# A transformer forward pass in split float32: two matmuls (512 and 256 columns) in place of three (256 each) per weight tile in the transposed projections

## The chip, the cores and the metric

The kernel runs on one core of a Trainium2 chip. The metric is the device time of one execution in microseconds; a time is the median of several executions. TensorE multiplies, VectorE and ScalarE move results out of the accumulator banks (PSUM) and do the element work, GpSimd does small numerics, and SyncE (SP) issues the loads of the weights.

## What is computed

256 tokens of 2048 channels pass through two attention layers (one with an index-selected key set, one plain causal), a block that mixes sparse attention (NSA) with a gated delta rule, and a gated feed-forward network (FFN). All is float32. Nearly all the work is projections, activations times a weight matrix that is read once. The ones that the change touches are marked:

```python
gate = h @ w_in[:, 3072:5120]                 # touched, in both attention layers
h = h + (silu(gate) * o) @ w_out
proj = rms_norm(h, norm1_w) @ w_in_2          # touched: delta rule's q, k, v and the merge gates
mixed = g_nsa * (o_nsa @ w_up_nsa) + g_dn * (o_dn @ w_up_dn)     # touched, both
x = h + mixed @ w_o
h2 = rms_norm(x, norm2_w)
x = x + (silu(h2 @ w_ffn_gate) * (h2 @ w_ffn_up)) @ w_ffn_down   # touched: gate and up
```

## The kernel before

Activations are kept transposed, 128 channels on the partitions, in blocks of 4 x 128 channels by 256 tokens, and each block twice: `hi`, rounded to the matmul's float32r, and `lo`, what the rounding left. The weights stream through once. For each 1 MB load `raw` (512 rows by 512 columns, three buffers, issued by SP at L134) ScalarE casts a half of it to `wh` (L139) and VectorE subtracts to get `wl` (L140); each has three buffers. A product is then high·high + low·high + high·low, three matmuls into one bank.

`gemm` (L121) has two forms. Unflipped, the activations are the stationary operand and 512 weight columns move (L155 to L157). Flipped (`flip=True`), a 128 x 128 tile of weights is stationary and 256 tokens move (L148 to L150), so that the result comes out transposed. A flipped call has two banks; each holds two blocks of 128 columns by 256 tokens, and at the end of the call each bank is evacuated by one VectorE instruction of 512 columns, a multiplication by a per-token row (L573, L1255, L1265, L1327, L1335) or, after the up-projections of the two mixers, an add-and-multiply (L1278, L1290). The tag `mm` has four banks, so that two calls overlap.

There are 52 flipped calls: 44 with four input blocks (8 attention gates, 6 for the delta rule's q, k, v, 8 merge gates, 11 FFN gates, 11 FFN ups) and 8 short ones with two (four each for `w_up_nsa_2` and `w_up_dn_2`). The FFN runs in three passes, over 4, 4 and 3 column blocks of its inner width; a pass is its gate and up calls, then unflipped down calls.

Other work (attention, top-k, delta rule, sparse attention) runs in generators that `tick` advances between the matmuls of the projections, and `defer` puts small pieces some ticks later. `need(name)` runs a generator to its end before the next line is written. A scheduler then orders each engine's queue, so the order on an engine is near to that of the code but not the same. On one engine the queue is worked off in order. `split_into` (L521) splits a result into `hi` and `lo`; `x_T` (L238) transposes a residual block for the next layer on TensorE (L219) and splits it (L233, L234); `row_of` (L166) spreads per-token factors over the partitions.

Of the kernel before, what the change touches and what calls it, by code (L numbers as in the profile page):

```python
# [11 lines left out]
F32 = mybir.dt.float32  # L12
F32R = mybir.dt.float32r
# [13 lines left out]
class Kern:  # L27
    """The whole forward pass; activations stay in SBUF, weights stream through once."""

    def __init__(self, ctx, tc, d, out, stop=None):  # L30
# [9 lines left out]
        self.flip = False  # L40
        self.finished = set()

# [4 lines left out]
    def ev(self, name, dt=F32):  # L47
        """evacuations of the projections, apart from the background's tiles"""
        return self.sb.tile([P, 512], dt, tag="ev", bufs=8, name=name)

    def slot(self, name, dt=F32):
        """a [128, 2, 512] tile in a slot of the split activations"""
        self.flip = not self.flip
        return self.sb.tile([P, 2, 512], dt, tag="hi" if self.flip else "lo", bufs=8, name=name)
# [20 lines left out]
    def defer(self, n, fn):  # L75
        """trace fn after n further ticks"""
# [15 lines left out]
    def tick(self):  # L92
        """advance deferred work and the background chains"""
# [27 lines left out]
    def gemm(self, xT, W, c0, n, evac, ng=4, split=False, flip=False):  # L121
# [3 lines left out]
        pt = [self.ps.tile([P, 512], F32, tag="mm", bufs=4, name="mm") for _ in range(2)]  # L125
        for g in range(ng):
# [8 lines left out]
            hi, lo = xT[g]  # L135
            for h in range(2):
                wh = self.sb.tile([P, 2, n], F32R, tag="wh", bufs=3, name="wh")
                wl = self.sb.tile([P, 2, n], F32R, tag="wl", bufs=3, name="wl")
                nc.scalar.copy(wh, raw[:, 2 * h:2 * h + 2])  # L139
                nc.vector.tensor_tensor(wl, raw[:, 2 * h:2 * h + 2], wh.bitcast(F32), ALU.subtract)  # L140
                for c in range(2):
# [1367 lines left out]
```

## Time and profile before

| | |
|---|---|
| runs | 2311.62, 2310.85, 2311.79 us; median 2311.62 |
| span of the profiled execution, first to last instruction | 2308.8 us |
| TensorE matmul / weight load busy | 2295.5 us (99%) / 2094.7 us (91%) |
| VectorE / ScalarE / GpSimd busy | 1395.8 us (60%) / 1089.4 us (47%) / 133.6 us (6%) |
| matmuls | 16446 |
| read from memory, mean rate | 397.95 MB, 174 GB/s over the span |

The page gives no other time for the profiled execution than its span; the runs are 2.1 to 3.0 us above it. A line of the profile names the engine, the line of the kernel, the operation, what it writes and reads, a count, the busy time and the mean of one; "PEld" is TensorE's load of stationary weights. A matmul is drawn from its start to the end of its passage through the array, and the next one begins before that, so a step from one matmul to the next is shorter than a matmul.

### The profile page before, as it was taken

To read this page: it belongs to the slowest core of one execution; us is meant where nothing else is said; L and a number is where in the kernel's file an instruction comes from. 1 tells how busy PE (TensorE), PEld (TensorE's weight loads), DVE (VectorE), ACT (ScalarE), POOL (GpSimd) and SP (SyncE) were. 2 spreads that over 40 slices of the span, in tenths; PEclk is the share of its full clock that TensorE was granted. 3 is DMA by queue.
4 is the path that set the end of the run, shared out by engine and by line. 5 is a ranking of instruction groups with operands and counts; after the bars stand their busy time and mean duration, and the time that the engine had idled before them with its cause. 6 is when DMAs were issued, how large, how long until landed. Compare 5 with 4: busy or idle time off the path is not lost.

```text
span 2308.8 us, 39431 instructions
## 1 busy us (share of the span) xinstructions
PE 2295.5 (99%) x16446; PEld 2094.7 (91%) x16446; DVE 1395.8 (60%) x2073; ACT 1089.4 (47%) x1758; POOL 133.6 (6%) x233
## 2 busy tenths in 40 slices
PE   9999999999999999999999999999999999999998
PEld 8878998888998888999999999889998899989997
DVE  5686765656665656878675655555555455554555
ACT  5555644456544434564534444454443344433444
POOL 1011100112100300011101000000000000000000
PEclk9999999999999999999999999999999999999999
DMA  7544455654556754344443665555555555555554
GB/s 230 193 149 153 140 183 182 189 176 137 167 183 208 240 157 152 112 164 130 146 148 120 205 225 183 182 192 191 183 183 189 192 184 183 183 182 184 182 185 143
DMA packets 209811, 404.70 MB, mean 175 GB/s; under 512 B 7376, under 2 KB 25776, under 8 KB 209632
## 3 DMA queue, kind: packets, MB, share of 16 engines
q1 hardware_dynamic: 206880, 394.04, 52.5%
q0 software_dynamic: 2752, 8.13, 1.2%
q8 instruction: 129, 2.11, 0.4%
q14 instruction: 50, 0.41, 0.1%
HBM read 397.95 MB, written 4.19 MB: 174 GB/s over the span
## 4 chain that ended last, share of the span: by engine, by line
PE 99%; DMA 0%; DVE 0%; SPq 0%; ACT 0%; issue 0%; ACTq 0%; POOLq 0%; POOL 0%
PE mm L150 16%; PE mm L148 16%; PE mm L149 16%; PE mm L157 14%; PE mm L156 14%; PE mm L155 14%; PE lg L440 1%; PE tr L294 1%; PE tp L219 1%; PE hid L994 1%; PE nl L1086 0%; PE pt L473 0%; PE ib L638 0%; DMA x<-in_x_dram 0%; PE ov L490 0%; PE ov L491 0%
## 5 line engine op out<-in xcount | busy, mean ns | idle before, releaser
L140 DVE TENSOR_TENSOR wl<-raw,wh 128x1024 fp32r<-128x1024 f32 (+4 forms) x760 | 902.6, 1188 | 794.2 <-ACT wh L139 793.1
L139 ACT CAST wh<-raw 128x1024 fp32r<-128x1024 f32 (+4 forms) x760 | 775.9, 1021 | 1028.5 <-PE mm L149 550.3
L150 PE MATMUL mm<-hi,wl 128*128 128x256 f32 x3072 | 868.9, 284 | 0.0
L148 PE MATMUL mm<-hi,wh 128*128 128x256 f32 x3072 | 868.4, 283 | 0.0
L149 PE MATMUL mm<-lo,wh 128*128 128x256 f32 x3072 | 868.1, 283 | 0.0
L148 PEld LDWEIGHTS mm<-hi,wh 128*128 128x128 f32 x3072 | 579.8, 189 | 1.5 <-issue 0.5
L149 PEld LDWEIGHTS mm<-lo,wh 128*128 128x128 f32 x3072 | 579.2, 189 | 0.8 <-issue 0.2
L150 PEld LDWEIGHTS mm<-hi,wl 128*128 128x128 f32 x3072 | 577.9, 188 | 1.0 <-issue 0.2
L156 PE MATMUL mm<-wl,hi 128*128 128x512 f32 (+4 forms) x1504 | 574.6, 383 | 0.2 <-DVE wl L140 0.2
L157 PE MATMUL mm<-wh,lo 128*128 128x512 f32 (+4 forms) x1504 | 570.6, 381 | 0.0
L155 PE MATMUL mm<-wh,hi 128*128 128x512 f32 (+4 forms) x1504 | 529.3, 382 | 0.0
L156 PEld LDWEIGHTS mm<-wl,hi 128*128 128x128 f32 x1504 | 283.3, 188 | 55.4 <-issue 0.6
L157 PEld LDWEIGHTS mm<-wh,lo 128*128 128x128 f32 x1504 | 283.1, 188 | 55.0 <-issue 1.5
L155 PEld LDWEIGHTS mm<-wh,hi 128*128 128x128 f32 x1504 | 281.1, 189 | 56.2 <-issue 1.3
L248 POOL TENSOR_SCALAR rsqv<-nsum 128x1 f32<-128x1 f32 x10 | 3.5, 351 | 1228.4 <-DVE nsum L1361 744.4
L233 ACT ACTIVATE hi<-tp,gT 128x256 fp32r<-128x256 f32 x64 | 27.6, 471 | 21.3 <-PE tp L219 18.9
L454 ACT ACTIVATE lg<-lg,nb 128x128 f32<-128x128 f32 (+1 forms) x64 | 28.4, 445 | 16.7 <-POOL nb L447 16.7
L234 DVE SCALAR_TENSOR_TENSOR lo<-tp,gT,hi 128x256 fp32r<-128x256 f32 x64 | 28.4, 478 | 12.4 <-ACT hi L233 12.0
L730 DVE SCALAR_TENSOR_TENSOR cv<-raw,cols,cv 128x255 f32<-128x255 f32 (+2 forms) x72 | 31.1, 475 | 1.8 <-ACT cv L727 1.7
L252 ACT ACTIVATE junk<-x 128x512 bf16<-128x512 f32 (+1 forms) x42 | 25.6, 610 | 6.0 <-DMA x<-in_x_dram 2.2
L252 ACT ACTIVATE junk<-mm 128x128 bf16<-128x128 f32 x80 | 22.2, 278 | 7.3 <-PE mm L157 5.8
L440 PE MATMUL lg<-kT,qT 128*128 128x256 f32 (+1 forms) x128 | 23.7, 327 | 0.0
(378 smaller groups left out, 1386.2 us busy)
## 6 DMA issues: line engine op xcount, KB each, us to landing
raw<-in_w_in_dram SPq DMA_DIRECT2D x76, 1024.0 KB, 5.1
raw<-in_w_ffn_gate_dram SPq DMA_DIRECT2D x44, 1024.0 KB, 5.2
raw<-in_w_ffn_up_dram SPq DMA_DIRECT2D x44, 1024.0 KB, 5.2
raw<-in_w_ffn_down_dram SPq DMA_DIRECT2D x41, 1024.0 KB, 5.1
raw<-in_a_w_in_dram SPq DMA_DIRECT2D x40, 1024.0 KB, 5.1
raw<-in_b_w_in_dram SPq DMA_DIRECT2D x40, 1024.0 KB, 5.1
raw<-in_a_w_out_dram SPq DMA_DIRECT2D x16, 1024.0 KB, 5.0
raw<-in_b_w_out_dram SPq DMA_DIRECT2D x16, 1024.0 KB, 5.1
```

Source lines behind the costliest of these rows:

```text
L139: nc.scalar.copy(wh, raw[:, 2 * h:2 * h + 2])
L140: nc.vector.tensor_tensor(wl, raw[:, 2 * h:2 * h + 2], wh.bitcast(F32), ALU.subtract)
L148: nc.tensor.matmul(o, wh[:, c, ms], hi[:, kc], start=first and m % 2 == 0, stop=False)
L149: nc.tensor.matmul(o, wh[:, c, ms], lo[:, kc], start=False, stop=False)
L150: nc.tensor.matmul(o, wl[:, c, ms], hi[:, kc], start=False, stop=last and m % 2 == 1)
L155: nc.tensor.matmul(o, xh, wh[:, c], start=first, stop=False)
L156: nc.tensor.matmul(o, xh, wl[:, c], start=False, stop=False)
L157: nc.tensor.matmul(o, xl, wh[:, c], start=False, stop=last)
L234: nc.vector.scalar_tensor_tensor(lo[:, k], tp[:, c], g, hi[:, k].bitcast(F32), ALU.mult, ALU.subtract)
L252: self.nc.scalar.activation(self.junk()[:, :w], in_, AF.Square, accum_out=accum)
L440: nc.tensor.matmul(lb[:, i * S:(i + 1) * S], qT[:, h * P:(h + 1) * P], kT[:, :S], start=True, stop=True)
L730: v.scalar_tensor_tensor(o[:, s:], x[:, :T - s], self.convw[:, k:k + 1], o[:, s:], ALU.mult, ALU.add)
```

## The change

A block now holds high and low side by side in one tile, `hl` [128, 4, 2, 256], so that high and low tokens of 128 channels are 512 neighbouring columns. A new function `gemm_T` takes the place of the flipped form. Per weight tile it does one matmul of 512 columns, `wh` against high and low together, and one of 256, `wl` against high. The first 256 columns of a bank then hold high·high + high·low of one block of 128 output columns, the other 256 hold low·high. So a bank holds one block instead of two, and a call goes through its columns in two halves of 256, each with two banks and its own evacuation in the middle or at the end of the call. A load is 1024 rows by 256 columns instead of 512 by 512, and a block of `wh` and `wl` is 4 chunks by 256 columns instead of 2 by 512. Before the evacuation each bank's halves are merged (`add_halves`): ScalarE copies the second half to SBUF, VectorE adds the first to it. In the short calls the merge has a tile of its own, `halves`, with one buffer. Temporary tiles that used the rooms of `hi` and `lo` now take halves of an `hl` tile (`slot`).

```diff
+    def gemm_T(self, xT, W, c0, evac, ng=4):
+        for b in range(2):
+            pt = self.banks()
+            for g2 in range(ng // 2):
+                self.flush(lambda: len(xT) > 2 * g2 + 1 and None not in xT[2 * g2:2 * g2 + 2])
+                raw = self.sb.tile([P, 8, T], F32, tag="raw", bufs=3, name="raw")
+                nc.sync.dma_start(raw, W[g2 * 1024:(g2 + 1) * 1024,
+                                         c0 + b * T:c0 + (b + 1) * T].rearrange("(c p) n -> p c n", p=P))
+                for h in range(2):
+                    wh, wl = self.weights(raw, h, T)
+                    hl = xT[2 * g2 + h][2]
+                    for c in range(4):
...
+                        for m in range(2):
+                            ms = slice(m * P, (m + 1) * P)
+                            nc.tensor.matmul(self.c2(pt[m]), wh[:, c, ms], hl[:, c],
+                                             start=first, stop=False)
+                            nc.tensor.matmul(pt[m][:, :T], wl[:, c, ms], hl[:, c, 0],
+                                             start=False, stop=last)
+                        if c % 2:
+                            self.tick()
+            evac(b, pt)
...
-                    for m in range(4 if flip else 0):
-                        o = pt[m // 2][:, (m % 2) * T:(m % 2 + 1) * T]
-                        ms = slice(m * P, (m + 1) * P)
-                        nc.tensor.matmul(o, wh[:, c, ms], hi[:, kc], start=first and m % 2 == 0, stop=False)
-                        nc.tensor.matmul(o, wh[:, c, ms], lo[:, kc], start=False, stop=False)
-                        nc.tensor.matmul(o, wl[:, c, ms], hi[:, kc], start=False, stop=last and m % 2 == 1)
...
+    def halves(self):
+        return self.sb.tile([P, T], F32, tag="halves", bufs=1, name="halves")
+
+    def add_halves(self, o, bank):
+        self.nc.scalar.copy(o, bank[:, T:])
+        self.nc.vector.tensor_tensor(o, bank[:, :T], o, ALU.add)
+
+    def joined(self, o, pt, row):
+        for i in range(2):
+            self.add_halves(o[:, i], pt[i])
+        self.nc.vector.tensor_tensor(o, o, row, ALU.mult)
...
     def new_T(self):
-        hi = self.sb.tile([P, 4, T], F32R, tag="hi", bufs=8, name="hi")
-        lo = self.sb.tile([P, 4, T], F32R, tag="lo", bufs=8, name="lo")
-        return hi, lo
+        hl = self.sb.tile([P, 4, 2, T], F32R, tag="hl", bufs=8, name="hl")
+        return hl[:, :, 0], hl[:, :, 1], hl
...
-                def evac_g(b, ps):
-                    v.tensor_tensor(s[b], ps, row, ALU.mult)
+                def evac_g(b, pt):
+                    self.joined(s[b], pt, row)
...
-            self.gemm(nT, d["w_up_nsa_2"][0], 512 * j, 512,
-                      lambda b, ps: v.scalar_tensor_tensor(m[b], m[b], 1.0, ps, ALU.add, ALU.mult),
-                      ng=2, flip=True)
+            def evac_n(b, pt, m=m):
+                for i in range(2):
+                    up, mi = self.halves(), m[b][:, i]
+                    self.add_halves(up, pt[i])
+                    v.scalar_tensor_tensor(mi, mi, 1.0, up, ALU.add, ALU.mult)
+            self.gemm_T(nT, d["w_up_nsa_2"][0], 512 * j, evac_n, ng=2)
```

Three places in the engines' queues. The first is TensorE in the first FFN gate call: two sets (a set is what one 128 x 128 weight tile needs). `mm_` numbers are banks, `hi_`, `lo_` and `hl_` blocks of the input. Before:

```order
L148 MATMUL mm_16115<-hi_15603,wh_16167 128x256
L149 MATMUL mm_16115<-lo_15604,wh_16167 128x256
L150 MATMUL mm_16115<-hi_15603,wl_16168 128x256
L148 MATMUL mm_16116<-hi_15603,wh_16167 128x256
L149 MATMUL mm_16116<-lo_15604,wh_16167 128x256
L150 MATMUL mm_16116<-hi_15603,wl_16168 128x256
```

And now:

```order
L189 MATMUL mm_14744<-hl_14398,wh_14787 128x512
L191 MATMUL mm_14744<-hl_14398,wl_14788 128x256
L189 MATMUL mm_14745<-hl_14398,wh_14787 128x512
L191 MATMUL mm_14745<-hl_14398,wl_14788 128x256
```

The two matmuls with `wh` have become one; L189 and L191 are lines of the changed kernel.

The second is VectorE at the evacuation of that call (`sg` is the gate's result). Before:

```order
L140 TENSOR_TENSOR wl_16408<-raw_16377,wh_16407 128x1024
L1327 TENSOR_TENSOR sg0_16113<-mm_16115,row_16096 128x512
L1327 TENSOR_TENSOR sg1_16114<-mm_16116,row_16096 128x512
L140 TENSOR_TENSOR wl_16438<-raw_16435,wh_16437 128x1024
```

And now:

```order
L207 TENSOR_TENSOR sg0_14742<-mm_14744,sg0_14742 128x256
L136 TENSOR_TENSOR wl_14922<-raw_14899,wh_14921 128x1024
L207 TENSOR_TENSOR sg0_14742<-mm_14745,sg0_14742 128x256
L136 TENSOR_TENSOR wl_14953<-raw_14950,wh_14952 128x1024
L213 TENSOR_TENSOR sg0_14742<-sg0_14742,row_14725 128x512
L136 TENSOR_TENSOR wl_14973<-raw_14950,wh_14972 128x1024
L207 TENSOR_TENSOR sg1_14743<-mm_14855,sg1_14743 128x256
L136 TENSOR_TENSOR wl_14995<-raw_14992,wh_14994 128x1024
L207 TENSOR_TENSOR sg1_14743<-mm_14856,sg1_14743 128x256
L213 TENSOR_TENSOR sg1_14743<-sg1_14743,row_14725 128x512
```

Both banks were evacuated at the call's end; now the first half's two merges and multiplication stand in the middle of the call, with subtractions for the next blocks between them. On ScalarE the copies (L206) stand likewise between casts.

The third is TensorE at the start of the FFN, where the last residual block is transposed (L219, now L269) after the projection that completes it. `x03_` and `x13_` are the two halves of that residual block. Before, its transposes stood five matmuls into the third input block of the call's four (`hi_15767`, 48 matmuls):

```order
L148 MATMUL mm_16115<-hi_15767,wh_16197 128x256
L149 MATMUL mm_16115<-lo_15768,wh_16197 128x256
L150 MATMUL mm_16115<-hi_15767,wl_16198 128x256
L148 MATMUL mm_16115<-hi_15767,wh_16197 128x256
L149 MATMUL mm_16115<-lo_15768,wh_16197 128x256
L175 MATMUL row_16095<-diag_16097,ones_83 128x128
L219 MATMUL tp_16149<-ident_74,x03_14192 128x128
```

Now they stand five sets into the third block (`hl_14561`, eight sets). The rows from the last transpose on, with `mm_14855` and `mm_14856` the banks of the call's second half:

```order
L269 MATMUL tp_14778<-ident_74,x13_13058 128x128
L189 MATMUL mm_14745<-hl_14561,wh_14809 128x512
L191 MATMUL mm_14745<-hl_14561,wl_14810 128x256
L189 MATMUL mm_14744<-hl_14561,wh_14809 128x512
L191 MATMUL mm_14744<-hl_14561,wl_14810 128x256
L189 MATMUL mm_14745<-hl_14561,wh_14809 128x512
L191 MATMUL mm_14745<-hl_14561,wl_14810 128x256
L189 MATMUL mm_14855<-hl_14235,wh_14859 128x512
L189 MATMUL mm_14856<-hl_14235,wh_14859 128x512
```

And eight sets later, where `hl_14768`, the new block, is first used:

```order
L189 MATMUL mm_14855<-hl_14235,wh_14859 128x512
L191 MATMUL mm_14855<-hl_14235,wl_14860 128x256
L189 MATMUL mm_14856<-hl_14235,wh_14859 128x512
L191 MATMUL mm_14856<-hl_14235,wl_14860 128x256
L189 MATMUL mm_14744<-hl_14768,wh_14829 128x512
L191 MATMUL mm_14744<-hl_14768,wl_14830 128x256
L189 MATMUL mm_14745<-hl_14768,wh_14829 128x512
L191 MATMUL mm_14745<-hl_14768,wl_14830 128x256
```

The scheduler has put one block of the second half ahead of the first use of the new block; after the transposes come three sets of the third block, these eight, then the new block.

## Rows read from the trace of the kernel before

**Rows 1.** The page, parts 1 and 4: busy shares, and the chain that ended last.

```profile
PE 2295.5 (99%) x16446; PEld 2094.7 (91%) x16446; DVE 1395.8 (60%) x2073; ACT 1089.4 (47%) x1758; POOL 133.6 (6%) x233
...
PE 99%; DMA 0%; DVE 0%; SPq 0%; ACT 0%; issue 0%; ACTq 0%; POOLq 0%; POOL 0%
```

**Rows 2.** Waits of TensorE: who waited, for whom, total us, times, longest.

```profile
PE warm L311 <- DVE zero L308: 1.7, 1, 1.7
PE gt L320 <- DMA g<-in_a_norm_dram: 1.3, 1, 1.3
PE tp L219 <- DMA x<-in_x_dram: 1.0, 1, 1.0
PE mm L156 <- DVE wl L140: 0.2, 1, 0.2
```

**Rows 3.** Busy time by stretch: length, each engine's busy us (count), PEclk, DMA share, GB/s.

```profile
1294.00:1455.00 161.00, 161.00 (x1360) 161.00 (x1359) 89.83 (x92) 68.62 (x75) 0.00 (x0) 1.00 0.59 197
...
1730.96:1820.18 89.22, 89.22 (x386) 72.37 (x385) 46.15 (x45) 34.81 (x34) 0.00 (x0) 1.00 0.57 189
1820.18:2004.50 184.32, 184.32 (x1537) 184.31 (x1536) 96.04 (x93) 75.07 (x78) 0.00 (x0) 1.00 0.57 183
2004.50:2094.09 89.59, 89.59 (x386) 72.11 (x385) 46.17 (x45) 34.80 (x34) 0.00 (x0) 1.00 0.56 188
2094.09:2232.33 138.24, 138.24 (x1153) 138.22 (x1152) 71.49 (x69) 55.97 (x58) 0.00 (x0) 1.00 0.57 183
2282.53:2299.39 16.86, 16.86 (x144) 16.86 (x143) 11.84 (x25) 9.76 (x22) 0.76 (x2) 1.00 0.29 94
1000.00:1200.00 200.00, 200.00 (x2482) 196.39 (x2482) 149.67 (x261) 96.97 (x181) 19.80 (x36) 1.00 0.44 143
```

**Rows 4.** Groups by line and form: the flipped matmuls, the weights' subtraction and cast.

```profile
L150 PE MATMUL mm<-hi,wl 128*128 128x256 f32 x3072 | 868.9, 284 | 0.0
L148 PE MATMUL mm<-hi,wh 128*128 128x256 f32 x3072 | 868.4, 283 | 0.0
...
L140 DVE TENSOR_TENSOR wl<-raw,wh 128x1024 fp32r<-128x1024 f32 x698 | 853.8, 1223 | 741.7 <-ACT wh L139 741.0 <-issue 0.2
...
L139 ACT CAST wh<-raw 128x1024 fp32r<-128x1024 f32 x698 | 732.6, 1050 | 957.2 <-PE mm L149 544.2 <-PE mm L157 393.9 <-issue 11.1
```

**Rows 5.** Loads: queue, count, KB each, median us from issue to landing.

```profile
raw<-in_w_ffn_gate_dram SPq DMA_DIRECT2D x44, 1024.0 KB, 5.2
...
raw<-in_w_ffn_down_dram SPq DMA_DIRECT2D x41, 1024.0 KB, 5.1
...
raw<-in_w_ffn_down_dram SPq DMA_DIRECT2D x6, 512.0 KB, 3.4
```

**Rows 6.** Waits of SP's queue: the longest.

```profile
SPq L134 <- DVE wl L140: 1814.5, 334, 11.8
```

**Rows 7.** Groups by line and form: PSUM copies, additions and multiplications like the merges'.

```profile
L493 ACT COPY o<-ov 128x256 f32<-128x256 f32 x32 | 11.1, 374 | 13.9 <-PE ov L491 13.6
...
L283 DVE TENSOR_TENSOR rope<-mm,tabs 128x256 f32<-128x256 f32 x40 | 15.0, 413 | 0.0
...
L285 DVE SCALAR_TENSOR_TENSOR rope<-mm,rstd,rope 128x256 f32<-128x256 f32 x8 | 3.5, 474 | 0.0
...
L573 DVE TENSOR_TENSOR gt<-mm,row 128x512 f32<-128x512 f32 x16 | 11.0, 689 | 0.3 <-PE mm L150 0.2
```

**Rows 8.** Timeline of ScalarE and VectorE, first attention layer: last attention output; two gates' evacuations.

```profile
271.27 0.37 ACT L493 COPY o<-ov 128x256 f32<-128x256 f32 x1 [1.85 <-PE ov L491]
...
305.45 1.41 DVE L573 TENSOR_TENSOR gt<-mm,row 128x512 f32<-128x512 f32 x2
...
328.24 1.41 DVE L573 TENSOR_TENSOR gt<-mm,row 128x512 f32<-128x512 f32 x2
```

**Rows 9.** Timeline at the FFN's start: residual addition, transposes, last low part.

```profile
1547.01 1.28 DVE L532 TENSOR_TENSOR x<-mm,x 128x512 f32<-128x512 f32 x2
...
1553.88 1.04 PE L219 MATMUL tp<-ident,x 128*128 128x128 f32 x8
...
1556.99 0.48 DVE L234 SCALAR_TENSOR_TENSOR lo<-tp,gT,hi 128x256 fp32r<-128x256 f32 x1
```

More of the change, by code (lines that the diff above doesn't have):

```diff
@@ L39, in __init__ @@
         self.later = []
-        self.flip = False
+        self.half = None
         self.finished = set()
@@ L51, in slot @@
     def slot(self, name, dt=F32):
-        self.flip = not self.flip
-        return self.sb.tile([P, 2, 512], dt, tag="hi" if self.flip else "lo", bufs=8, name=name)
+        if self.half is not None:
+            b, self.half = self.half, None
+        else:
+            t = self.sb.tile([P, 2, 2, 512], F32, tag="hl", bufs=8, name="half")
+            b, self.half = t[:, 0], t[:, 1]
+        return b if dt is F32 else b.bitcast(dt)
     def pair(self, name, dt=F32):
@@ L118, in ready, with banks, weights, gemm @@
             yield
-    def gemm(self, xT, W, c0, n, evac, ng=4, split=False, flip=False):
+    def banks(self):
+        return [self.ps.tile([P, 512], F32, tag="mm", bufs=4, name="mm") for _ in range(2)]
+    def weights(self, raw, h, n):
         nc = self.nc
-        pt = [self.ps.tile([P, 512], F32, tag="mm", bufs=4, name="mm") for _ in range(2)]
+        k = raw.shape[1] // 2
+        wh = self.sb.tile([P, k, n], F32R, tag="wh", bufs=3, name="wh")
+        wl = self.sb.tile([P, k, n], F32R, tag="wl", bufs=3, name="wl")
+        nc.scalar.copy(wh, raw[:, k * h:k * h + k])
+        nc.vector.tensor_tensor(wl, raw[:, k * h:k * h + k], wh.bitcast(F32), ALU.subtract)
+        return wh, wl
+    def gemm(self, xT, W, c0, n, evac, ng=4, split=False):
+        nc = self.nc
+        pt = self.banks()
         for g in range(ng):
@@ L134, in gemm @@
                 nc.sync.dma_start(raw, src)
-            hi, lo = xT[g]
+            hi, lo, _ = xT[g]
             for h in range(2):
[L137 to L140, printed above, removed]
+                wh, wl = self.weights(raw, h, n)
                 for c in range(2):
@@ L159, in gemm @@
         for t in range(2):
[L160 removed]
+            evac(t, pt[t][:, :n])
+    def gemm_T(self, xT, W, c0, evac, ng=4):
+        nc = self.nc
+        for b in range(2):
+            pt = self.banks()
+            for g2 in range(ng // 2):
[7 more added lines that the diff above has]
+                    for c in range(4):
+                        first = g2 == 0 and h == 0 and c == 0
+                        last = g2 == ng // 2 - 1 and h == 1 and c == 3
+                        for m in range(2):
[7 more added lines that the diff above has]
+            evac(b, pt)
     @staticmethod
@@ L192, in gemm_by_tile @@
                 ws.append((wh, wl))
+        pt = self.banks()
         for t in range(2):
-            o = self.ps.tile([P, 512], F32, tag="mm", bufs=4, name="mm")[:, :n]
+            o = pt[t][:, :n]
             ts = slice(t * P, (t + 1) * P)
             for g in range(ng):
-                hi, lo = xT[g]
+                hi, lo, _ = xT[g]
                 for c in range(4):
```

52 lines of the change are left out of this document (27 added, 25 removed).

## The prediction

> **What bounds the kernel now.** I read the page first: its busy shares and its chain [rows 1]. TensorE is busy 99% of a span of 2308.8 us and the chain that ended last is 99% TensorE; VectorE has 60%, ScalarE 47%. TensorE's own waits come next [rows 2]: four in the whole span, 4.2 us together, none for a PSUM bank. So the time is the sum of TensorE's steps from matmul to matmul. I then looked at stretches that hold projections of one kind only [rows 3]. A matmul's own duration (283 ns) is no step, because the next one starts before it ends, so I divide a stretch by its matmuls, which the loops give (a window also counts the one or two that straddle its edge). Flipped, 256 columns each: 161.00 us for some 1,358 is 118.6 ns; in the second and third FFN pass 184.32 / 1536 and 138.24 / 1152 are 120.0 ns. Unflipped, 512 columns each: 89.22 / 384 = 232.3 ns, and 89.59 / 384 = 233.3 ns in the second pass. Two steps of 256 columns take 237.2 ns where one of 512 takes 232.3: an instruction of its own costs about 5 ns. The granted clock is 1.00 in all these stretches.
>
> The three runs have a median of 2311.6 us, 2.8 above the span; what lies around the span I leave as it is, and forecast against 2311.6.
>
> **The change part by part.**
>
> *Matmuls.* A set, one 128x128 tile of weights against all 256 tokens, was three matmuls of 256 columns (high·high, low·high, high·low); there are 3072 of each [rows 4]. Now it is one of 512 and one of 256. The columns stay 768, one matmul and one weight load go. No row shows a 512 followed by a 256, so I bound the new set. Above: 3 x 118.6 = 355.8 ns, no gain; a loss is not to be had here, since a 256-column step already hides a weight load of its own and a 512-column one hides it with room. Below: 768 columns at 232.3/512 ns each, 348.5 ns. Between them lies the plain sum of the two steps, 232.3 + 118.6 = 350.9 ns, which I take, since both steps stand in the rows. That saves 4.9 ns a set; in the later two FFN passes 3 x 120.0 - (233.3 + 120.0) = 6.7 ns. Those passes hold (1536 + 1152) / 3 = 896 sets, the rest 2176: 2176 x 4.9 + 896 x 6.7 = 10.7 + 6.0 = **16.7 us**.
>
> The tail, 256 columns with hardly anything beside it, shows 16.86 / 143 = 117.9 ns [rows 3], so part of the 118.6 belongs to what runs beside; with it the saving is 2 x 117.9 - 232.3 = 3.5 ns, 10.8 us in all. That is a rival below. The Trainium skill (TensorE: Matmul & The Clock Gate, "Back-to-back issue gap") puts the warm gap at N/2.4 + 2.5 ns. By it a matmul less saves 2.5 ns, 3072 x 2.5 = 7.7 us, and the estimate is 2304. The trace disagrees on the gaps: it has 118.6 and 232.3 ns where that rule gives 109.2 and 215.8.
>
> *Weights.* A block is 1024 columns as before (four chunks by 256 instead of two by 512), as many blocks as before: the cast of 1.05 us and the subtraction of 1.22 us [rows 4] keep number and size. A block now lasts TensorE 8 sets, 2.8 us, where 24 matmuls took 2.85. Both engines still fit under it with 1.6 us to spare: nothing.
>
> *Loads.* As many, 1 MB each, but in 1 KB pieces instead of 2 KB. 1 MB in 2 KB pieces lands after 5.1 us, 512 KB in 1 KB pieces (256 columns of the last gemms) after 3.4 [rows 5]. So 1 MB in 1 KB pieces takes from 5.1 to 6.8 us. One load feeds 5.6 us of matmuls, there are three buffers, and SP waits 1814.5 us in 334 waits for a subtraction to free a buffer [rows 6], so a load is issued as soon as it can be, some 11 us ahead of its use: nothing, at either end.
>
> *Merges.* 52 calls in two halves of two banks are 208 merges, each a ScalarE copy of 256 columns out of PSUM and a VectorE addition of 256. Such a copy takes 374 ns, such an addition 413 [rows 7]: 78 us more on ScalarE (to 51%) and 86 on VectorE (to 64%). The multiplication by the row stays at 512 columns (689 ns). None of it is on TensorE's path while a bank pair is free in time. There are four banks; a half of a long call lasts 32 sets, 11.2 us, one of a short call (8 calls with two input blocks) 5.6 us, and that is the time the merges of the half before it have. The longest chain is in the short calls, where one buffer serves both merges: copy, add, use, twice, 2 x (0.37 + 0.41 + 0.47) = 2.5 us, plus one cast and one subtraction that stand between, 1.05 + 1.22, is 4.8 us. It fits by 0.8 us. Behind the ScalarE copy, which waits for the bank's last matmul, the next cast is queued, but that cast waits for the same matmul, whose block it overwrites. Under 0 nothing is to be had; above, 16 short halves late by 1 us each are 16 us. Half of them fall in the stretch where VectorE also has the delta rule (149.67 of 200 us busy [rows 3]). I take **2 us**, near the lower end, because TensorE waits for no bank today and the order lets work of the next half go ahead.
>
> *Earlier needs.* Evacuating the first half of a gate call needs the attention of its group 11 us sooner. The last attention output of the layer is copied out at 271.6 us; its gate call ran from 306 to 328 us [rows 8], so its half ends near 317: nothing. At the start of the FFN the last input block is needed after 24 sets (8.4 us) instead of after 17 us. Its transposes ran 6.9 us after the residual addition began and its low parts were done 10.5 us after it [rows 9], which would cost up to 10.5 - 8.4 = 2.1 us. But in TensorE's new order three sets of the block before and eight of the call's second half stand between the transposes and the first use, 3.9 us, where 3.6 us passed from the transposes to the last low part: nothing. The eight need the second half's first load early; it is the third of the three buffers, issued when the call begins.
>
> Sum: -16.7 + 2 = -14.7, **2297 us**.
>
> **The rivals.**
> - *Weight loads bind the 256-column stream.* There TensorE's load slot is busy 184.31 of 184.32 us, in the 512-column one 72.37 of 89.22 [rows 3]. With a third of the loads gone a set would then cost only its columns, 348.5 ns: 7.3 x 3072 = 22 us, 2289 us. Against it: the last row of 256 has as full a slot and a shorter step. The Trainium skill (Trainium Kernel Development and Optimization, "Best Practices") judges TensorE by this busy share and not by matmul busy time; the trace has the share at full, so the rule speaks for this rival. Chance 0.10.
> - *The step saves less*, 3.5 ns a set, because 118.6 holds disturbance that stays: 10.8 us less 0 to 2, 2301 to 2303 us. For it: the tail's 117.9. The rule of the issue gap gives nearly this time. Chance 0.12.
> - *The banks come late.* Each of the 16 short halves waits 1 us for the merges of the half two before: the 16.7 us are given back, 2311 us. It decides when the chain of 4.8 us passes 5.6, that is with two background operations of VectorE in it. Chance 0.12.
> - *Slower: VectorE's queue in the second block.* The delta rule's matmuls stand in TensorE's queue and wait for VectorE results. 22 calls there bring 88 merges; if each addition of 0.41 us delays such a result and TensorE has no projection ahead of it, 36 us come on top of -16.7: 2331 us. It decides if VectorE, at 75% there, becomes so late that TensorE's queue runs into it; 28 merges per 200 us bring it to 81%. Against it: 50 us in 200 are idle now. Chance 0.08.
>
> **How the numbers follow.** The forecast has 0.58; with the two rivals on the gaining side 0.80 is on one side, and the range takes these in: from 2289 less 3 for a sharper second pass to 2303 with another 4 us of bank waits, **2286 to 2307**. What a measurement can tell from no change is 0.2%, 4.6 us. Faster by more: forecast and the first two rivals, 0.80. Within: late banks, 0.12. Slower: 0.08.
>
> **What would show it.** Some 13,400 matmuls instead of 16,446. In an FFN gate stretch, a set every 351 ns; near 348 speaks for the load slot, near 352.5 for the smaller step. Wait rows on TensorE that name the merges' additions, most of all around the short calls, would show the banks; gaps in front of the delta rule's small matmuls the last rival. VectorE near 1480 us, ScalarE near 1165. I am wrong if a set in an undisturbed stretch takes 356 ns or more, or if TensorE's waits sum to over 15 us.

## The result, and the profile after the change

The changed kernel takes **2295.49 us** (median of four runs, 2295.19 to 2295.85) where the kernel before takes 2311.65 (2310.85 to 2311.79): a ratio of 0.9931, 95% interval 0.9917 to 0.9945. The forecast was 2297, the range 2286 to 2307. The span of the profiled execution fell from 2308.8 to 2293.4 us, by 15.4.

The page of the changed kernel, busy shares and the chain that ended last (with [rows 1]):

```profile
PE 2276.4 (99%) x13374; PEld 1939.6 (85%) x13374; DVE 1480.4 (65%) x2297; ACT 1146.2 (50%) x1966; POOL 136.0 (6%) x233
...
PE 98%; DVE 1%; ACT 0%; DMA 0%; issue 0%; SPq 0%; POOL 0%; ACTq 0%; POOLq 0%
```

3072 matmuls are gone, VectorE has 84.6 us more and ScalarE 56.8. TensorE is still the bound. Its waits (with [rows 2]):

```profile
PE tp L269 <- DMA x<-in_x_dram: 2.7, 2, 2.5
PE warm L361 <- DVE zero L358: 1.7, 1, 1.7
PE ov L539 <- ACT half L527: 1.3, 1, 1.3
PE mm L189 <- DVE raw L207: 1.2, 1, 1.2
PE mm L189 <- DVE gt L207: 0.8, 1, 0.8
```

Two of them are new and name an addition of the merges (L207), 2.0 us together; neither lies in a short call. A third is new and names a cast of the first layer's attention (L527). Stretches of one kind of projection (with [rows 3]; columns as there): FFN pass 1 in its middle, pass 2 gates and ups, pass 2 down, pass 3 gates and ups.

```profile
1570.00:1700.00 130.00, 130.00 (x743) 113.88 (x742) 81.08 (x94) 61.44 (x81) 0.00 (x0) 1.00 0.59 189
1814.14:1993.74 179.60, 179.60 (x1026) 157.32 (x1024) 109.53 (x125) 84.17 (x110) 0.00 (x0) 1.00 0.58 188
1993.74:2082.27 88.53, 88.53 (x383) 71.79 (x382) 45.04 (x43) 34.60 (x35) 0.00 (x0) 1.00 0.58 190
2082.97:2217.66 134.69, 134.69 (x769) 117.97 (x768) 81.72 (x93) 62.85 (x82) 0.00 (x0) 1.00 0.58 188
```

The second row holds 512 sets, the fourth 384: 179.60 / 512 = 350.8 ns and 134.69 / 384 = 350.8 ns a set. The load slot has idle time now (157.32 of 179.60). The groups by line and form (with [rows 4, 7]):

```profile
L189 PE MATMUL mm<-hl,wh 128*128 128x512 f32 x3072 | 1076.4, 395 | 2.0 <-DVE raw L207 1.2 <-DVE gt L207 0.8
L191 PE MATMUL mm<-hl,wl 128*128 128x256 f32 x3072 | 850.1, 284 | 0.1
...
L207 DVE TENSOR_TENSOR sg<-mm,sg 128x256 f32<-128x256 f32 x44 | 18.5, 421 | 15.5 <-ACT sg L206 15.5
...
L206 ACT COPY sg<-mm 128x256 f32<-128x256 f32 x44 | 16.4, 372 | 32.1 <-PE mm L191 32.1
```

and a load (with [rows 5]):

```profile
raw<-in_w_ffn_gate_dram SPq DMA_DIRECT2D x44, 1024.0 KB, 5.1
```

Where the 15.4 us came from: I take the starts of the same unflipped matmuls in both traces as stage marks. Relative to the kernel before, the changed one is

| stage | change, us | by the measured sets |
|---|---|---|
| up to the end of layer 1's query projections | +0.6 | no sets |
| layer 1's four gates (256 sets) | +2.4 | -1.3 |
| layer 2's four gates (256 sets) | -1.4 | -1.3 |
| second block (1152 sets) | -5.0 | -6.0 |
| FFN pass 1 (512 sets) | -2.7 | -2.7 |
| FFN pass 2 (512 sets), then its down projections | -4.7, -0.4 | -4.7 |
| FFN pass 3 (384 sets) | -3.6 | -3.5 |
| the last stretch after it | -0.7 | no sets |

The column on the right is (356.0 - 350.8) = 5.2 ns a set, and 360.0 - 350.8 = 9.2 ns in passes 2 and 3, where a set took three times the 120.0 ns of [rows 3]. Together it is -19.6 us; the losses are 3.7 in layer 1's gates, 1.0 in the second block and 0.6 at the start. The 0.7 us at the end I did not follow up.

### The profile page after: what moved, and what is told of

The parts are those of the page before. It is cut to its first block, busy times and chain, and to the rows that moved or that the text cites. A ratio compares the mean times of both kernels' runs of the same rounds, so it can differ in the third digit from the quotient of the medians.

```text
span 2293.4 us, 33719 instructions
## 1 busy us (share of the span) xinstructions
PE 2276.4 (99%) x13374; PEld 1939.6 (85%) x13374; DVE 1480.4 (65%) x2297; ACT 1146.2 (50%) x1966; POOL 136.0 (6%) x233
## 4 chain that ended last, share of the span: by engine, by line
PE 98%; DVE 1%; ACT 0%; DMA 0%; issue 0%; SPq 0%; POOL 0%; ACTq 0%; POOLq 0%
PE mm L189 31%; PE mm L191 16%; PE mm L163 14%; PE mm L164 14%; PE mm L165 14%; PE lg L490 1%; PE tr L344 1%; PE tp L269 1%; PE hid L1044 1%; PE pt L523 0%; PE ib L688 0%; PE nl L1136 0%; DMA x<-in_x_dram 0%; DVE wl L136 0%; PE ov L540 0%; PE cvb L791 0%
## 5 line engine op out<-in xcount | busy, mean ns | idle before, releaser
L189 PE MATMUL mm<-hl,wh 128*128 128x512 f32 x3072 | 1076.4, 395 | 2.0 <-DVE raw L207 1.2
L191 PE MATMUL mm<-hl,wl 128*128 128x256 f32 x3072 | 850.1, 284 | 0.1
L189 PEld LDWEIGHTS mm<-hl,wh 128*128 128x128 f32 x3072 | 568.9, 188 | 122.6 <-DVE raw L207 1.4
L191 PEld LDWEIGHTS mm<-hl,wl 128*128 128x128 f32 x3072 | 576.9, 188 | 12.6 <-DVE wl L136 0.4
L164 PE MATMUL mm<-wl,hl 128*128 128x512 f32 (+4 forms) x1504 | 574.4, 383 | 0.2 <-DVE wl L136 0.2
L165 PE MATMUL mm<-wh,hl 128*128 128x512 f32 (+4 forms) x1504 | 570.0, 381 | 0.0
L163 PE MATMUL mm<-wh,hl 128*128 128x512 f32 (+4 forms) x1504 | 529.6, 382 | 0.0
L164 PEld LDWEIGHTS mm<-wl,hl 128*128 128x128 f32 x1504 | 283.5, 189 | 55.2 <-issue 0.6
L165 PEld LDWEIGHTS mm<-wh,hl 128*128 128x128 f32 x1504 | 283.1, 188 | 55.1 <-issue 1.5
L163 PEld LDWEIGHTS mm<-wh,hl 128*128 128x128 f32 x1504 | 281.4, 189 | 56.5 <-issue 1.3
L283 ACT ACTIVATE hl<-tp,gT 128x256 fp32r<-128x256 f32 x64 | 27.6, 471 | 22.1 <-PE tp L269 20.0
L284 DVE SCALAR_TENSOR_TENSOR hl<-tp,gT,hl 128x256 fp32r<-128x256 f32 x64 | 28.5, 478 | 12.7 <-ACT hl L283 12.5
L206 ACT COPY up<-mm 128x256 f32<-128x256 f32 x44 | 16.4, 373 | 32.3 <-PE mm L191 32.3
L206 ACT COPY sg<-mm 128x256 f32<-128x256 f32 x44 | 16.4, 372 | 32.1 <-PE mm L191 32.1
L207 DVE TENSOR_TENSOR sg<-mm,sg 128x256 f32<-128x256 f32 x44 | 18.5, 421 | 15.5 <-ACT sg L206 15.5
L207 DVE TENSOR_TENSOR up<-mm,up 128x256 f32<-128x256 f32 x44 | 18.5, 421 | 13.5 <-ACT up L206 13.5
```

The source lines that it names most:

```text
L163: nc.tensor.matmul(o, xh, wh[:, c], start=first, stop=False)
L164: nc.tensor.matmul(o, xh, wl[:, c], start=False, stop=False)
L165: nc.tensor.matmul(o, xl, wh[:, c], start=False, stop=last)
L189: nc.tensor.matmul(self.c2(pt[m]), wh[:, c, ms], hl[:, c], start=first, stop=False)
L191: nc.tensor.matmul(pt[m][:, :T], wl[:, c, ms], hl[:, c, 0], start=False, stop=last)
L206: self.nc.scalar.copy(o, bank[:, T:])
```

## The experiments

Theory A is the prediction's: the gain lies in the number of matmuls. The differences below are against the changed kernel, unless the kernel before is named. Beside the experiments the kernel before took 2311.19 us (the first four), 2311.32 (the next four) and 2310.74 (the last three), beside the changed kernel 2311.65; so a difference of 1 us against the changed kernel's total says little, and a trace has to tell where it arises. Line numbers are each kernel's own.

**Old matmuls, new layout.** Everything as changed, merges included, but high·high and low·high as two matmuls again.

```diff
-    nc.tensor.matmul(self.c2(pt[m]), wh[:, c, ms], hl[:, c], start=first, stop=False)
+    nc.tensor.matmul(pt[m][:, :T], wh[:, c, ms], hl[:, c, 0], start=first, stop=False)
+    nc.tensor.matmul(pt[m][:, T:], wh[:, c, ms], hl[:, c, 1], start=False, stop=False)
     nc.tensor.matmul(pt[m][:, :T], wl[:, c, ms], hl[:, c, 0], start=False, stop=last)
```

> The changed kernel with one thing put back: a set is three matmuls of 256 columns again (high.high into the first half of the bank, low.high into the second, high.low into the first); halves, banks, loads, merges and evacuations stay as changed. Theory A (a matmul costs about 5 ns of its own and the change gains by having one less): a set takes 3 x 118.7 = 356 ns, or 360 where the step is 120 as in the two later FFN passes of before, against 350.8 now, so 5.2 x 3072 = 16 us to 9.2 x 3072 = 28 us more than the changed kernel: 2311 to 2324 us. Rival B (the gain came from the new layout of loads, blocks and halves, or from a different order of the queues): within 4 us of the changed kernel, 2292 to 2300 us. If the later passes show 120 again, that state belongs to the pattern of three matmuls; if not, to the old layout.

2315.2 us (2314.11 to 2315.67); against the kernel before 1.0017, 1.0008 to 1.0026. Theory A holds: without the wide matmul all of the gain goes. (A matmul that goes takes its weight load with it; no run here parts the two.) What is left of the change, layout and merges with the order that they bring, costs 4.0 us against the kernel before, and nothing in the FFN. The middle of pass 1, and pass 2, of this kernel:

```profile
1570.00:1700.00 130.00, 130.00 (x1098) 130.00 (x1097) 79.63 (x92) 62.18 (x81) 0.00 (x0) 1.00 0.57 186
1825.35:2009.67 184.32, 184.32 (x1538) 184.32 (x1536) 109.60 (x125) 84.08 (x110) 0.00 (x0) 1.00 0.56 183
```

184.32 us for pass 2 is to the hundredth what the kernel before takes without merges [rows 3]. In the timeline of this pass the steps repeat 117, 120, 123 ns without any spread, 360.0 ns a set; in pass 1 they vary between 115 and 122 and average 118.7. The exact 360 also appears in the later part of both attention layers' gates here, where the kernel before has 356.0 on average; that is some 360 sets, 1.4 of the 4.0 us. So it belongs to three equal matmuls, not to the old layout.

**No merges.** The evacuations read only the first half of a bank; low·high is left out of the result.

```diff
 def joined(self, o, pt, row):
     for i in range(2):
-        self.add_halves(o[:, i], pt[i])
-    self.nc.vector.tensor_tensor(o, o, row, ALU.mult)
+        self.nc.vector.tensor_tensor(o[:, i], pt[i][:, :T], row[:, i], ALU.mult)
...
-    up, mi = self.halves(), m[b][:, i]
-    self.add_halves(up, pt[i])
-    v.scalar_tensor_tensor(mi, mi, 1.0, up, ALU.add, ALU.mult)
+    mi = m[b][:, i]
+    v.scalar_tensor_tensor(mi, mi, 1.0, pt[i][:, :T], ALU.add, ALU.mult)
```

> The changed kernel without the merges: no copy and no addition, the evacuation reads the first half of each bank alone (low.high is computed and left out). Theory A (merges cost only the few waits that the trace shows on TensorE, 2.0 us for banks, and 1.7 us of late attention in the first layer): 2 to 5 us less, 2290 to 2294 us, and the waits on the additions gone. Rival C (the merges cost nothing, the first layer lost its 3.7 us by the shared rooms of the temporary tiles): within 1 us of the changed kernel, 2294.5 to 2296.5 us. Rival D (the merges hold up the second block's chain of small matmuls): over 8 us less, under 2288 us.

2294.41 us (2293.29 to 2297.53), 1.1 less than with merges, within the spread of its own runs: between the bands of theory A and rival C, 0.1 us from C's; rival D (over 8 us less) falls. Its TensorE waits no longer name an addition, but the one on the attention's cast stays:

```profile
PE xz L917 <- issue: 1.7, 1, 1.7
...
PE ov L538 <- ACT half L526: 1.3, 1, 1.3
```

So the 208 merges show no cost beyond their two bank waits (2.0 us), as far as runs that spread over 4 us can tell. Most of layer 1's loss is not theirs: the stretch from the last query projection to the first output matmul takes 108.9 us here and 110.1 with merges, so 1.3 of the 3.7 us go with them and 2.4 stay.

**Two matmuls of 384 columns.** 768 columns a set as before, evenly split; low·high is left out for half of the tokens, low·low comes in for the other half. (The merge's copy takes columns 128 to 383 of a bank, so it keeps its size.)

```diff
-    nc.tensor.matmul(self.c2(pt[m]), wh[:, c, ms], hl[:, c], ...)
-    nc.tensor.matmul(pt[m][:, :T], wl[:, c, ms], hl[:, c, 0], ...)
+    x = hl[:, c].rearrange("p c n -> p (c n)")[:, :384]
+    nc.tensor.matmul(pt[m][:, :384], wh[:, c, ms], x, ...)
+    nc.tensor.matmul(pt[m][:, :384], wl[:, c, ms], x, ...)
...
-        self.nc.scalar.copy(o, bank[:, T:])
+        self.nc.scalar.copy(o, bank[:, P:384])
```

> The changed kernel with its two matmuls of a set at 384 columns each instead of 512 and 256; the same count of matmuls, of weight loads and of columns. Both take the first 384 of the 512 columns, so low.high is left out for half of the tokens and a superfluous low.low is added for them. Theory A (columns at one rate plus a fixed cost for each matmul): a set takes 350.8 ns as now, 2294 to 2297 us. Rival E (the weight load binds the 256-column step, a 384-column one is free of it): 768 columns at 0.4537 ns, 348.5 ns a set, 7 us less, 2288 us.

2302.62 us (2301.96 to 2303.85): slower by 7.1, a miss for both. In FFN pass 2

```profile
1819.36:1999.58 180.22, 180.22 (x1025) 180.22 (x1024) 109.57 (x125) 84.18 (x110) 0.00 (x0) 1.00 0.57 187
```

a set takes 180.22 / 512 = 352.0 ns, 1.2 more than with 512 + 256. Here too the steps repeat a fixed pattern, 174, 175, 182, 176, 173 ns. In the merge gates of the same kernel (1306 to 1450 us) it is another, 174 to 178 ns, and a step averages 175.55, a set 351.1; so most of the 1.2 comes with the pattern, and theory A's set stands where its time fails. Two loads under even matmuls do not bring the column price of 348.5, so the load slot is not shown as the bound. The other 3.4 us were lost in layer 1 and the second block; one stretch in layer 1, 240 to 250 us, has a granted clock of 0.83, a part of it at the lower of the two levels, 1.2 GHz, and the rest at 2.4.

**Four matmuls.** High·high and low·high as two matmuls of 256 columns and high·low as two of 128, so that a set has four loads for the same 768 columns.

```diff
-    nc.tensor.matmul(self.c2(pt[m]), wh[:, c, ms], hl[:, c], ...)
-    nc.tensor.matmul(pt[m][:, :T], wl[:, c, ms], hl[:, c, 0], ...)
+    nc.tensor.matmul(pt[m][:, :T], wh[:, c, ms], hl[:, c, 0], ...)
+    nc.tensor.matmul(pt[m][:, T:], wh[:, c, ms], hl[:, c, 1], ...)
+    nc.tensor.matmul(pt[m][:, :P], wl[:, c, ms], hl[:, c, 0, :P], ...)
+    nc.tensor.matmul(pt[m][:, P:T], wl[:, c, ms], hl[:, c, 0, P:], ...)
```

> The changed kernel with four matmuls in a set: high.high and low.high of 256 columns each and high.low in two of 128 columns. Columns stay 768, weight loads become four. It measures what bounds a short step. Theory A (fixed cost of about 5 ns, 0.444 ns a column) alone would give a 128-column step of about 62 ns and a set of 361 ns, 2326 us. If a weight load needs its own time that 128 columns do not cover, the 128-column step shows that time; the transposes' steps of about 90 ns suggest 90, a set of 417 ns, 2500 us. Rival E (the load binds the 256-column step at 118.6) needs 118 for the 128-column step too: a set of 474 ns, 2675 us.

2611.6 us (one run). Pass 2 of this kernel:

```profile
2038.49:2270.58 232.09, 232.09 (x2049) 232.09 (x2048) 110.17 (x125) 83.51 (x110) 0.00 (x0) 1.00 0.45 146
```

453.3 ns a set, 113.3 ns a matmul on average though half of them have only 128 columns: between what A and E gave. In the timeline the starts of the four matmuls are 172, 113, 58 and 111 ns apart, those of the loads nearly even, 108 to 124. Here the loads do bind, at a pace of 113 ns, just under the 118.7 of the 256-column step. The transposes, 128 columns each, fit that: they step by 109 ns in the kernel before and in the changed one, and not by the 90 that I had put into the expectation. By the column price (232.3 / 512 ns) 113.3 ns is the time of 250 columns, an estimate; so at 256 the load is close to being the bound and is not yet. A load's record is 188 ns long and overlaps the next one's; loads 113 ns apart and loads 120 ns apart both show a full slot.

**Another order.** The two long matmuls of a chunk's two output blocks first, then the two short ones.

```diff
     for m in range(2):
         nc.tensor.matmul(self.c2(pt[m]), wh[:, c, ms], hl[:, c], start=first, stop=False)
+    for m in range(2):
+        ms = slice(m * P, (m + 1) * P)
         nc.tensor.matmul(pt[m][:, :T], wl[:, c, ms], hl[:, c, 0], start=False, stop=last)
```

> The changed kernel with another order inside a chunk: the two 512-column matmuls of the two output blocks first, then the two of 256 columns. Numbers of instructions and columns are unchanged. Theory A (a step has the length of its own matmul, 232.3 or 118.6 ns, whatever stands beside it): the four steps of two sets still take 701.7 ns, the kernel 2294 to 2297 us. Rival F (what a step costs depends on the neighbour: a long matmul hides the next weight load with room, a short one hardly): with two short ones behind each other the pair of sets takes longer, up to 2 x 356 = 712 ns, 2311 us; or the regular beat of equal matmuls (120.0 for 118.7, 233.3 for 232.4 ns) comes back: 706.6 ns, 2303 us.

2295.18 us (2294.40 to 2296.65), the time that theory A gave, but not for its reason. Pass 2:

```profile
1816.18:1994.56 178.38, 178.38 (x1025) 156.12 (x1024) 108.16 (x125) 83.29 (x109) 0.00 (x0) 1.00 0.59 189
```

178.38 / 512 = 348.4 ns a set, the price of the columns alone. The four steps average 227.6, 234.6, 116.3 and 118.3 ns: what a step costs depends on its neighbours, as rival F has it, but it gets shorter and not longer. The gain (2.3 us in the FFN's first two passes, 0.9 in the third, about 1 in the attention gates) was given back: the kernel starts 0.5 us later and loses 3.6 in the second block. There TensorE waits for a cast up to 963.86 us and for a VectorE result up to 1237, and the granted clock is 0.83 from 960 to 970 us (behind the first wait some 512-column steps take 0.43 us, at 1.2 GHz, and then 0.24 again), where the changed kernel has 1.00:

```profile
PE nov L1192 <- ACT half L1177: 2.0, 1, 2.0
...
PE z L910 <- DVE X L922: 1.1, 1, 1.1
```

```profile
960.00:970.00 10.00, 8.03 (x34) 5.73 (x33) 8.24 (x30) 5.70 (x17) 2.15 (x3) 0.83 0.34 106
```

**Layer 1: rate, and three matmuls there alone.** Two ways to move the attention's pieces in the queues. `rate` sets how fast `tick` advances them; in the other kernel `dsa` is true in the first layer alone, and `three` brings back the three matmuls of the first experiment in its gates.

```diff
-        self.rate = {"a": 0.7}
+        self.rate = {"a": 0.8}
```

> The changed kernel with the background's rate in the attention layers at 0.8 instead of 0.7, so that the attention pieces come earlier into the queues. Theory G (the 3.7 us lost in the first layer's gates come from the place at which the scheduler happened to put the attention's casts on ScalarE, not from the merges as such): the stretch from the end of the last query projection to the first output matmul, 110.1 us in the changed kernel, moves by 1 us or more in either direction, and TensorE's wait of 1.3 us for ScalarE's cast goes or moves; total 2290 to 2300 us. Rival H (the merges and their bank waits cost this in any order): the stretch stays within 0.5 us of 110.1, total 2295 to 2296.

```diff
-            self.gemm_T(hT, w_in, cg + 512 * g, evac)
+            self.gemm_T(hT, w_in, cg + 512 * g, evac, three=dsa)
```

> The changed kernel with the old three matmuls of 256 columns a set in the four gate calls of the first attention layer alone (256 sets); merges, layout and all else as changed. ScalarE's queue there then stands as it did before the change. Theory G (queue order): the wait of 1.3 us for the cast goes, the stretch takes what it took with three matmuls everywhere, 108.5 us instead of 110.1: the kernel is 1 to 2 us faster than the changed one, 2293.5 to 2294.5, although 256 sets cost 5.2 ns more each (1.3 us). Rival H (merges cost it in any order): the stretch takes 110.1 + 1.3 = 111.4 us, the kernel 2296.5 to 2297.

With rate 0.8: 2293.81 us (2292.09 to 2295.33; the profiled execution is the fastest of the five). The stretch from the last query projection to the first output matmul takes 100.8 us instead of 110.1, because 6 us of attention now lie ahead of it; up to its end the kernel is 3.2 us earlier, 0.4 of it from the start, the wait for the cast is gone and another of 2.4 us has come (`mm L163 <- DVE vl L600`). With three matmuls in layer 1: 2292.97 us (2292.89 to 2294.04), 0.5 us under theory G's band, and the stretch takes 108.5, as G has it. (In the kernel before it takes 107.7; 0.7 of the 0.8 us between are some 170 sets at 360.0 ns instead of 356.0.) Theory G holds in both, rival H in neither. ScalarE in the kernel before, in the changed kernel, then in the one with three matmuls:

```profile
239.78 0.59 ACT L477 CAST pT<-pt 128x512 fp32r<-128x512 f32 x1 [0.21 <-PE pt L473]
240.27 1.05 ACT L139 CAST wh<-raw 128x1024 fp32r<-128x1024 f32 x1
```

```profile
239.23 1.05 ACT L135 CAST wh<-raw 128x1024 fp32r<-128x1024 f32 x1
240.18 0.27 ACT L302 ACTIVATE junk<-mm 128x128 bf16<-128x128 f32 x1
...
240.44 0.57 ACT L527 CAST half<-pt 128x512 fp32r<-128x512 f32 x1
```

```profile
239.82 0.59 ACT L533 CAST half<-pt 128x512 fp32r<-128x512 f32 x1 [0.21 <-PE pt L529]
240.30 1.05 ACT L135 CAST wh<-raw 128x1024 fp32r<-128x1024 f32 x1
```

In the changed kernel the attention's cast stands behind the weights' cast, and TensorE waits for it:

```profile
241.07 0.50 PE L539 MATMUL ov<-half,vh 128*128 128x512 f32 x1 [1.32 <-ACT half L527]
...
261.36 0.50 PE L189 MATMUL mm<-hl,wh 128*128 128x512 f32 x1 [0.81 <-DVE gt L207]
```

In the last it stands ahead, as it did before the change, with the merges in place. So with the 512-column matmuls the scheduler chose another order in this stretch; that it goes by their other durations is likely and not shown. The marked waits are 2.1 of the 3.7 us; the rest is in steps that I did not take apart.

**A shift in the kernel before.** Three equal matmuls, old code; in each gate and up call of passes 2 and 3 one matmul has 128 columns instead of 256 (low·high left out for half of the tokens in one tile); `nudge` is true in these calls.

```diff
+    n2 = P if nudge and g == 1 and kc == 0 and m == 0 else T
-    nc.tensor.matmul(o, wh[:, c, ms], lo[:, kc], start=False, stop=False)
+    nc.tensor.matmul(o[:, :n2], wh[:, c, ms], lo[:, kc, :n2], start=False, stop=False)
```

> The kernel before the change with one matmul of each gate and up call of the second and third FFN pass cut from 256 to 128 moving columns (14 matmuls; low times high is left out for half of the tokens in one weight tile a call), in order to shift the beat of the steps behind it by some 60 ns. Saved columns alone: 14 x 0.06 = 0.8 us. Theory I (the exact 360.0 ns a set in these passes is a phase in which equal matmuls settle, and it depends on where a stretch begins): after a shift some of the 14 calls run at 356.0 ns, others stay at 360.0; all 896 sets at 356.0 would save 3.6 us: 2307 to 2310 us. Rival J (it belongs to these passes, to their loads or their place in the program): all calls stay at 360.0 ns, 2310.5 us.

2307.06 us (2306.57 to 2308.18), 0.9982 of the kernel before, 0.9973 to 0.9991. Passes 2, its down projections, and 3:

```profile
1820.63:2002.91 182.28, 182.28 (x1537) 182.28 (x1536) 95.82 (x93) 75.07 (x78) 0.00 (x0) 1.00 0.57 185
2002.91:2091.43 88.52, 88.52 (x383) 71.80 (x382) 45.47 (x44) 34.81 (x34) 0.00 (x0) 1.00 0.57 190
2092.13:2228.85 136.72, 136.72 (x1153) 136.72 (x1152) 71.33 (x69) 55.99 (x58) 0.00 (x0) 1.00 0.57 185
```

Before the first shift a set takes 360.0 ns in the timeline; with it the 512 sets of pass 2 take 182.28 / 512 = 356.0 ns on average, those of pass 3 136.72 / 384 = 356.0. (The cut matmuls themselves save next to nothing: the step from a cut one to the next matmul takes 58 ns and the step after it 172, together 230, which fits two loads at a pace of 113 ns or a little more.) The down projections of pass 2, which nothing touched, go from 233.3 ns a step [rows 3] to 88.52 / 381 = 232.3 (the window ends at the start of their last set). Theory I holds more fully than expected: behind its shift every one of the 14 calls runs at some 356.0. But a shift does not take the beat away for good. Pass 3 begins in it again, eight sets in 2.88 us, 360.0 ns each, up to its own first shift at 2098.0 us:

```profile
2095.00 0.28 PE L148 MATMUL mm<-hi,wh 128*128 128x256 f32 x1
...
2097.88 0.28 PE L148 MATMUL mm<-hi,wh 128*128 128x256 f32 x1
```

So the 4 ns a set are a phase that a shift ends, not a cost of those passes. Rival J is not wholly out: both passes begin in the phase here, in the kernel before and in the first experiment, and why is open. The shift alone is worth 4.3 us against the kernel before (2311.32); of the 16.2 us of the change some 4.0 are the end of this phase, 3.6 in 896 sets and 0.4 in the down projections of pass 2.

**Both improvements together.** The other order outside the second block, where it had lost time, and outside layer 1 (`pairs`: layer 2's gates and the FFN, 1664 sets), and one or both of the remedies for layer 1.

```diff
-                self.gemm_T(h2, d["w_ffn_gate_2"][0], 512 * jb, evac_g)
+                self.gemm_T(h2, d["w_ffn_gate_2"][0], 512 * jb, evac_g, pairs=True)
...
-            self.gemm_T(hT, w_in, cg + 512 * g, evac)
+            self.gemm_T(hT, w_in, cg + 512 * g, evac, three=dsa, pairs=not dsa)
```

Rate 0.8, no `three`:

> The changed kernel with the background's rate at 0.8 and the order 512, 512, 256, 256 in the second attention layer's gates and in the FFN's gate and up calls (256 + 1408 = 1664 sets), the second block as changed. If the gains of the two experiments add: rate 0.8 measured 2293.8 us; the other order measured 348.3 ns a set instead of 350.8 in undisturbed stretches, 1664 x 2.5 = 4.2 us: 2289.7 us, 2288.5 to 2291. If the shorter set only moves work into a wait (as in the second block of the run with this order everywhere): 2292 to 2294.

Rate 0.7 with `three`, as in the diff:

> The changed kernel with three matmuls of 256 columns a set in the first attention layer's gates (256 sets) and the order 512, 512, 256, 256 in the second layer's gates and the FFN (1664 sets), the second block as changed, rate 0.7. If the gains add: 2293.0 - 4.2 = 2288.8 us, 2288 to 2290.5. If not: 2292 to 2293.

Rate 0.8 with `three`:

> As the run before, with the background's rate at 0.8 as well. Theory G (both edits of the first layer do the same thing, they put the attention's casts where TensorE does not wait for them, so that they do not add; and three matmuls cost 1.3 us more there): about 1 us slower than the run with rate 0.8 alone in that place, 2289 to 2291 us. If they add, 2287 us or less.

2290.82 (2288.10 to 2291.20), **2290.23** (2289.98 to 2290.63) and 2291.78 us (2289.92 to 2292.81). The second is 0.9910 of the kernel before (0.9896 to 0.9924), and its runs are the steadiest of the three; it is 5.3 us under the changed kernel, some 4.3 when each is taken against its own runs of the kernel before. The first two times lie in the bands in which the gains add. The two remedies for layer 1 do not add, as theory G says; the third kernel came out 0.8 us above the band given for that. The second kernel's waits hold no attention cast any more:

```profile
PE tp L280 <- DMA x<-in_x_dram: 3.7, 1, 3.7
PE warm L372 <- DVE zero L369: 1.7, 1, 1.7
PE mm L195 <- DVE raw L218: 1.2, 1, 1.2
```

## Why the prediction was right, step by step

- **What bounds the kernel**: right. The chain is TensorE's before and after, and, layer 1's gates apart, the gain follows the number of sets to within 1 us a stage.
- **The set**: predicted 350.9 ns as 232.3 + 118.6, measured 350.8 in passes 2 and 3. The reason was too simple: the two steps are 230.8 and 120.0 in pass 2, with the same two kinds of matmul a set takes 348.4 in another order, and two of 384 columns take 351.1 or 352.0. The sum of two steps is a good estimate, and was no law.
- **The saving, 16.7 us**: the term that was mis-sized, by 2.9 us; the sets gave 19.6. In passes 2 and 3 I let the new kernel keep the 233.3 and 120.0 ns that I saw there and took 6.7 ns a set. I had read these as a property of the passes. The shift showed them to be a phase of equal matmuls that one of another length ends, and the changed kernel does not have it in any of the stretches looked at: 9.2 ns. In the other 2176 sets 5.2 ns came, 4.9 were predicted.
- **The merges, 2 us**: 2.0 us of bank waits, right in size and wrong in place. None is in the short calls, whose chain I had fitted with 0.8 us to spare; one is at a delta rule projection, one at a first-layer gate. Without merges the time is 1.1 us less, within the spread. VectorE came out at 1480 us as forecast, ScalarE at 1146 and not 1165: the 208 copies take the 370 ns expected, but in the records neighbouring instructions of ScalarE overlap (the cast at 239.23 above ends 0.10 us after the next one has begun), so its busy time grew by 57 us and not by 78.
- **Weights, loads, earlier needs, 0**: right. A load in 1 KB pieces lands after 5.1 us, the low end of the 5.1 to 6.8; nothing on TensorE waits for it, and FFN pass 1 gained all that its sets give. The FFN's start, with two halves of a call interleaved, cost nothing.
- **What was missing, 3 to 4 us**: the same work in another order. The prediction asked of each new instruction what it delays, and not whether the scheduler would put old instructions elsewhere. In layer 1 it put an attention cast behind a weight cast. That loss and the larger saving nearly cancel; that the total was closer than its terms is luck.
- **The rivals.** The load slot: fell, 2289 us did not come, though the set of 348.5 that it named is reachable by order. The Trainium skill (Trainium Kernel Development and Optimization, "Best Practices") judges TensorE's distance to its limit by MFU (the share of the peak arithmetic rate) and the load slot's busy share, not by matmul busy time; of the share the trace disagrees here, for the slot is full at 120.0 ns a load (184.32 of 184.32 us, first experiment) and as full at 113.3 (232.09 of 232.09, four matmuls), so a full slot was not yet the bound. The smaller step: fell, the saving was larger; the rule of the Trainium skill's "Back-to-back issue gap" (TensorE: Matmul & The Clock Gate) would have given 2304. That page calls its formula the gap of an isolated matmul and says that a stream of loads and matmuls has another pace, so I had used it where it does not claim to hold. Late banks: right as a mechanism at two places of some 100, and not at 16. The slower case: the second block gained 5.0 us of the 6.0, so VectorE's queue cost about 1 us net, not 36.

## What to carry to other kernels

Where TensorE is busy all the time, count matmul instructions as well as columns: one of 512 for two of 256, and with it one weight load, saved 5 ns each time here, and it paid for a copy and an addition per bank because these lay beside it. When durations change, compare the engines' order around every place where the old kernel had no slack; a cast one place further back cost TensorE a wait of 1.3 us, all the merges together 2.0. And before a stretch's step is taken as its property, look whether its steps have any spread: a beat with none can be a phase that the change will end.

## What the runs showed of the hardware that was not expected

- **A phase of equal matmuls.** Rows of equal matmuls run at 118.7, 175.5 or 232.4 ns a step (256, 384, 512 columns), or at exactly 120.0, 176.0 or 233.3 with a fixed pattern. A whole stretch is in one or the other; one matmul of another length ended the exact one for the rest of its stretch, and a later stretch began in it again. Alternating 512 and 256 was not seen in it. What sets the beat is open; no run here tells.
- **A step depends on its neighbours.** In the order 512, 512, 256, 256 the steps are 227.6, 234.6, 116.3, 118.3 ns, 348.4 a set; alternating it is 350.8.
- **A gap can cost more than itself.** In two kernels with rate 0.8 TensorE waits the same 2.39 us, up to 144 and 145 us. In the one with rate 0.8 alone the granted clock stays 1.00, 2.4 GHz; in the one with the other order as well it is 0.83 over the 10 us around the wait. There it falls to 1.2 GHz behind the wait: eight 512-column steps take 0.43 us instead of 0.23, and TensorE comes out 1.5 us later. In the third kernel with that rate it falls as well. The row of the second one:

```profile
140.00:150.00 10.00, 7.61 (x32) 5.42 (x29) 8.97 (x20) 7.35 (x27) 2.79 (x5) 0.83 0.34 107
```

At the start of the changed kernel the same happens behind the 2.5 us wait for the input:

```profile
10.00:20.00 10.00, 9.46 (x51) 9.20 (x52) 7.68 (x15) 9.53 (x25) 0.05 (x1) 0.83 1.07 375
```

The same window of the kernel before reads 1.00, but it is no proof of a full clock there. Its 368-column steps take 0.31 us up to 13.6 us and 0.17 behind, as those of the changed kernel do up to 14.4 us and behind, so it too ran the first of them at the lower level:

```profile
12.45 0.51 PE L155 MATMUL mm<-wh,hi 128*128 128x368 f32 x1
12.76 0.51 PE L156 MATMUL mm<-wl,hi 128*128 128x368 f32 x1
...
14.02 0.33 PE L155 MATMUL mm<-wh,hi 128*128 128x368 f32 x1
14.18 0.33 PE L156 MATMUL mm<-wl,hi 128*128 128x368 f32 x1
```

How long the wait for the input is differs from one execution to the next (1.0 to 4.1 us over the profiled runs here), so differences of 1 to 2 us at the start say nothing of a change.
